# Fused decoder layer: the down projection's sums in three lanes of tiles on ScalarE's queue

## The chip, the cores and the metric

The kernel is one program on one core of a Trainium2 chip. The metric is the device time of one execution in microseconds (us); lower is better. The engines are TensorE (PE in the profile; PEld its weight loads), VectorE (DVE), ScalarE (ACT), GpSimd (POOL) and SyncE (SP). Each engine works through its own instructions in the order in which the program gives them. DMAs are issued by an engine's queue (here nearly all by SP's); the issuing engine passes on to its next instruction when the DMA is out, and a DMA whose data must first be ready holds up what stands behind it on that engine.

## The reference

One decoder layer for T = 1024 tokens of D = 1024 features in fp32:

```python
mod = silu(c) @ w_ada + b_ada                     # six vectors: shift, scale, gate, twice (AdaLN)
u = x * (1 + scale_m) + shift_m
y = mixer(u)                                      # window attention + dilated attention, gated, then @ w_o
x = layer_norm(ALPHA * x + (1 + gate_m) * y)
u = x * (1 + scale_f) + shift_f
h = u @ w_gate_up                                 # 1024 x 5632: hg, hu of 2816 columns each
y = (silu(hg) * hu) @ w_down                      # 2816 x 1024
x = layer_norm(ALPHA * x + (1 + gate_f) * y)
```

The change lies in the last part, from `w_o` (its last residual sums) on.

## The kernel before

**Matrix products.** A product in fp32 is made of three matmuls of split operands (high x high, high x low, low x high). Weights arrive in fp32 by DMA; `split` makes the halves: ScalarE copies to `w_hi` (L144), VectorE subtracts to get `w_lo` (L145). TensorE's matmuls of such a product are at L1037 (`product`, `mac`).

**Stages around the change.** After the attention, the product with `w_o` writes eight banks of PSUM, one for each block of 128 rows, for the first 512 columns; `residual` (L1321) adds `x` to each on VectorE. The needed parts of `x` (tiles `xr`) are loaded by SP: four ahead, and each of the other four (`fetch_x`, L1318) when a `residual` has freed its tile. Then come the other 512 columns, the first layer norm, and the gate-and-up projection.

**Gate and up.** 22 pairs (a block of 128 columns of `hg` and the one of `hu`) are computed with Strassen and Winograd's scheme: seven products of 12 matmuls each instead of eight (the products are steps i = 0 to 6 of the loop over a pair p). Of pairs 0 to 3 two products were made ahead. A pair's weights are two tiles `r1`, `r2` of 512 KB (loaded by SP at L112, two pairs ahead); GpSimd makes sums of them (L126 to L132). `g_prepare(n + 3)` splits the weights of two products ahead. Results go through a few elementwise steps: ScalarE copies a bank (L1604, L1610) and applies Silu (L1616), VectorE adds and multiplies (L1614, L1620, L1621), GpSimd adds (L1618), and SP stores the two halves of the pair's `h` to `h_d` in DRAM (L1623, at i = 6). GpSimd also applies the first norm's `gain` (L1366, L1367) at the end of pairs 3 to 10.

**The sums for the down projection.** It uses the same scheme: seven products of 11 units (j), each unit 12 matmuls (L1655: four banks, three matmuls each). It needs sums of blocks of `w_down` and of `h`: 22 sets, 11 of either kind. A set (`sum_set`) loads two tiles of 512 KB (from `w_down` or from `h_d`, L1514, SP's queue), does four VectorE operations in two steps (L1520 to L1524 for `w_down`, L1526 to L1530 for `h`) and stores the tiles to DRAM (`wt2_d` or `hs_d`, L1534; the trace says `wt_d`, `hs_d`). It is a generator: each `yield` gives the work back until the next product. There are two lanes with tiles of their own, lane 0 with `a_raw` and `a_lo` from pair 8 on, lane 1 with `gb` from pair 11 on:

```python
def sums_ahead(p, i):
    for lane, first in enumerate((8, 11)):
        if i == 1 and p >= first and sets and (sets[0][0] == "w" or 2 * sets[0][1] + 1 < p):
            ...
            lanes[lane] = sum_set(*sets.pop(0), *tiles)
        next(lanes[lane], None)
```

So both lanes start a set at the same step, i = 1, of each pair; the loads go out there, the first two operations come two products later, the other two one later again, and the stores two products after those. One last set is done in the down projection itself.

**AdaLN.** `last_ada` makes the last gate vector in pairs 2 and on: 512 KB of `w_ada` into `a_raw` (L1486, SP), and at the next call VectorE adds it up (L1489, L1491). It is called at four of a pair's seven products.

**Down projection.** A unit's two operands (`dn_load`, 256 KB each, L1562 and L1564, SP) are split (`dn_prepare`; L169 on ScalarE, L170 on VectorE) and multiplied. The raw tiles are the buffers of `r1` and `r2`. In the last pair of gate and up, `dn_prepare(2 * i, ...)` splits the first units at every product from i = 1 on. After each product `dn_add` (L1649 and the line behind it) adds four banks into the rows `zt`, and `half_stats` gathers their statistics. Products 0, 2, 4 and 6 write the same four banks (`bank_a`); 1 has four others, and 3 and 5 share four more. During product 6, the last, the second layer norm is applied to rows 0 to 3 (`norm_shared`, whose second part is the returned `finish`), then to rows 4 to 7 as they get done; `norm_quick(7)` ends the program.

The order of instructions on each engine is that in which this code issues them. In the listings below `waits DMAHW3` means that an instruction waits for one of eight counters by which hardware DMAs report that they have landed; the DMAs take them in turn, whatever queue they are on. `x2` means twice in a row.

Of the kernel before, what the change touches and what calls it, by code (L numbers as in the profile page):

```python
# [18 lines left out]
P = 128  # L19
T = 1024  # L20
# [129 lines left out]
def decoder_layer(ctx: ExitStack, tc: tile.TileContext, I, out, dbg=None):  # L150
# [1165 lines left out]
    def fetch_x(tb, eh, pool):  # L1316
        xr_t[tb, eh] = pool.tile([P, 512], F32, name="xr", tag="half" if eh == 0 else "r", bufs=XB[eh])
        nc.sync.dma_start(xr_t[tb, eh], I["x"][tb * P:(tb + 1) * P, eh * 512:(eh + 1) * 512])  # L1318

    def residual(ps, tb, eh):  # L1320
        nc.vector.scalar_tensor_tensor(zrow(tb)[:, eh * 512:(eh + 1) * 512], xr_t.pop((tb, eh)), ALPHA, ps,  # L1321
                                       op0=OP.mult, op1=OP.add)
# [12 lines left out]
    for tb in range(NB):
        residual(banks[tb], tb, 0)
        if tb + XB[0] < NB:
            fetch_x(tb + XB[0], 0, mix)
    w_late = [ws.take(2) for _ in range(4)]
    ps2x.close()  # L1340
    ph2b.close()
# [140 lines left out]
    def last_ada():  # L1482
        acc5 = misc.tile([P, T], F32, name="gate5", bufs=1)
        for k in range(KC):
            raw = ev.tile([P, T], F32, name="a_raw", bufs=1)
            nc.sync.dma_start(raw, I["w_ada"][k * P:(k + 1) * P, 5 * D:])  # L1486
            yield
            if k == 0:
                nc.vector.tensor_scalar(acc5, raw, c_act[:, 0:1], None, op0=OP.mult)  # L1489
            else:  # L1490
                nc.vector.scalar_tensor_tensor(acc5, raw, c_act[:, k:k + 1], acc5, op0=OP.mult, op1=OP.add)  # L1491
            yield
        hl = [ev.tile([P, T], F32R, name=n, tag=n, bufs=1) for n in ("a_raw", "a_lo")]
        split(*hl, acc5)
        yield
        nc.sync.dma_start(acc5, I["b_ada"][:, 5 * D:].to_broadcast([P, D]))
        yield
        for t in range(2):
            s = slice(t * TH, (t + 1) * TH)
            ps = ps_x.tile([P, TH], F32, name="px")  # L1500
            for x in range(2):
                nc.tensor.matmul(ps, ones_r, hl[x][:, s], start=x == 0, stop=x == 1)
            nc.vector.tensor_tensor(acc5[:, s], ps, acc5[:, s], op=OP.add)
        nc.vector.tensor_scalar(acc5, acc5, 1.0, None, op0=OP.add)
        gates[5] = acc5

    ada = last_ada()
    NP = NF // 2
    sets = [(kind, j) for kind in "wh" for j in range(NP)]

    def sum_set(kind, j, x, y):
        for i, tile in enumerate((x, y)):
            f = 2 * j + i
            nc.sync.dma_start(tile, I["w_down"][f * P:(f + 1) * P, :] if kind == "w" else h_d[f])  # L1514
        yield
        yield
        x0, x1, y0, y1 = x[:, H0], x[:, H1], y[:, H0], y[:, H1]
        tt = nc.vector.tensor_tensor
        if kind == "w":
            tt(x0, x1, x0, op=OP.subtract)  # L1520
            tt(x1, y1, x1, op=OP.subtract)
            yield
            tt(y1, y1, x0, op=OP.subtract)
            tt(y0, y0, y1, op=OP.subtract)  # L1524
        else:
            tt(y1, x1, y1, op=OP.add)  # L1526
            tt(x1, x0, x1, op=OP.subtract)
            yield
            tt(x0, y1, x0, op=OP.subtract)
            tt(y0, y0, x0, op=OP.subtract)  # L1530
        yield
        yield
        for i, tile in enumerate((x, y)):
            nc.sync.dma_start((wt2_d if kind == "w" else hs_d)[j, 2 * i:2 * i + 2].rearrange("s p c -> p s c"),  # L1534
                              tile.rearrange("p (s c) -> p s c", s=2))
        yield

    lanes = [iter(()), iter(())]

    def sums_ahead(p, i):  # L1540
        for lane, first in enumerate((8, 11)):
            if i == 1 and p >= first and sets and (sets[0][0] == "w" or 2 * sets[0][1] + 1 < p):
                if lane == 0:
                    tiles = [ev.tile([P, T], F32, name=n, tag=n, bufs=1) for n in ("a_raw", "a_lo")]
                else:
                    gb = misc.tile([P, 2, D], F32, name="gb", tag="gb")
                    tiles = [gb[:, 0], gb[:, 1]]
                lanes[lane] = sum_set(*sets.pop(0), *tiles)
            next(lanes[lane], None)
# [4 lines left out]
    def dn_load(upto):  # L1554
        while len(dn_raw) < min(upto, DN):
            u = len(dn_raw)
            i, j = divmod(u, NP)
            raw = gx.tile([P, 2, TH], F32, name="dn", tag="r1" if u % 2 else "r2", bufs=2)
            dn_raw[u] = raw
            f = 2 * j + (i in (1, 5, 6))  # L1560
            rows = slice(f * P, (f + 1) * P)
            nc.sync.dma_start(raw[:, 0], {0: h_d[f][:, H0], 1: h_d[f][:, H0], 2: hs_d[j, 0], 3: hs_d[j, 3], 4: hs_d[j, 1],  # L1562
                                          5: hs_d[j, 2], 6: h_d[f][:, H1]}[i])
            nc.sync.dma_start(raw[:, 1], {0: I["w_down"][rows, H0], 1: I["w_down"][rows, H0], 2: wt2_d[j, 3], 3: wt2_d[j, 0],  # L1564
                                          4: wt2_d[j, 1], 5: I["w_down"][rows, H1], 6: wt2_d[j, 2]}[i])
# [10 lines left out]
    for p in range(NF):  # L1576
# [11 lines left out]
        for i in range(7):  # L1588
# [42 lines left out]
            else:  # L1631
                if i == 0:
                    dn_load(2)
                dn_prepare(2 * i, 2 if i < 4 else 4)
            sums_ahead(p, i)
            if p == 3 and i == 0:
                gb1 = norm_params(1)
            if p > 1 and i in (1, 3, 4, 6):
                next(ada, None)
            if i == 6 and 3 <= p < 3 + NB:  # L1640
                gain(p - 3, gb1)
# [18 lines left out]
        bst[tb] = st8[:, tb * 12:(tb + 1) * 12].rearrange("p (a b) -> p a b", a=2)  # L1660
    bank_a = [ps_f.tile([P, TH], F32, name="pf") for _ in range(4)]
    bank, ends = None, []
    last_set = sum_set(*sets.pop(0), *[ev.tile([P, T], F32, name=n, tag=n, bufs=1) for n in ("a_raw", "a_lo")])
    for i in range(6):
        if i in (1, 3):
            bank = [(ps_f, ps_x)[t // 2].tile([P, TH], F32, name=("pf", "px")[t // 2]) for t in range(4)]
        ps = bank if i % 2 else bank_a
        for j in range(NP):
            u = i * NP + j
            dn_prepare(u + 12, 4)  # L1670
            for t in range(4):
# [103 lines left out]
```

## Time and profile before

| | before |
|---|---|
| three runs, us | 1856.27, 1852.13, 1851.0 (median 1852.13) |
| profiled execution, us | 1854.48 |
| its span, us; mean granted clock | 1852.7; 0.982 |
| PE busy | 1783.3 (96%), 8774 matmuls |
| DVE, ACT, POOL busy | 1214.1 (66%), 843.3 (46%), 562.9 (30%) |
| DMA | 277.28 MB, 150 GB/s on average |
| chain that ended last | PE 73%, DVE 11%, DMA 7%, issue 3%, ACT 3%, SP's queue 2% |

The span runs from the first to the last recorded instruction; the execution's time holds some 2 us more. "Busy" counts an engine's own instructions, not the issuing of DMAs. The granted clock is the share of TensorE's full clock that it was allowed. The residual behind `w_o` lies near 1083 us of the span, pairs 3 to 21 of gate and up from 1199.65 to 1624.08, the down projection from there to 1833.5, and the last norms end at 1852.7. Rows of the trace give a time, a duration, engine, line and operation with output <- inputs; in brackets stands how long the engine had idled ahead of it and what ended that.

### The profile page before, as it was taken

How to read it: one execution, taken by the hardware profiler on the slowest of the kernel's cores; microseconds unless marked ns; L12 is line 12 of the kernel's file. 1: busy time of each engine (PE TensorE's matmuls, PEld its weight loads, DVE VectorE, ACT ScalarE, POOL GpSimd, SP SyncE). 2: the span in 40 equal slices, each digit the busy share in tenths (PEclk: the TensorE clock that was granted, in tenths of full speed). 3: DMA queues.
4: the chain of work that ended last, by engine and by line, in shares of the span. 5: the costliest groups of instructions: out<-in, count | busy, mean ns of one | idle time of the engine just before them, and what ended most of it. 6: DMA issues, size and time to landing. Idle time of an engine off the chain costs nothing.

```text
span 1852.7 us, 24551 instructions
## 1 busy us (share of the span) xinstructions
PE 1783.3 (96%) x8774; PEld 1458.4 (79%) x8774; DVE 1214.1 (66%) x2094; ACT 843.3 (46%) x1731; POOL 562.9 (30%) x357
## 2 busy tenths in 40 slices
PE   9999999999999999999999999999998889799995
PEld 7888888888888888788888878878777767688884
DVE  7655566557657766478558757766766666557668
ACT  6554444444445777654522227533333333344332
POOL 0232223323332322045026532456642223200003
PEclk9999999999999999999999999999999999899998
DMA  9322233234233322375756340343456666587542
GB/s 354 90 78 84 82 87 103 82 82 120 71 92 103 88 86 70 103 269 187 239 207 218 120 142 12 131 143 114 137 206 254 241 233 237 171 280 241 195 144 91
DMA packets 124058, 277.28 MB, mean 150 GB/s; under 512 B 17888, under 2 KB 27680, under 8 KB 123936
## 3 DMA queue, kind: packets, MB, share of 16 engines
q1 hardware_dynamic: 123328, 274.06, 44.3%
q8 instruction: 69, 1.13, 0.2%
q0 software_dynamic: 464, 1.58, 0.2%
q14 instruction: 53, 0.43, 0.1%
q10 hardware_dynamic: 144, 0.07, 0.0%
HBM read 203.99 MB, written 58.03 MB: 141 GB/s over the span
## 4 chain that ended last, share of the span: by engine, by line
PE 73%; DVE 11%; DMA 7%; issue 3%; ACT 3%; SPq 2%; POOL 1%; DVEq 0%; ACTq 0%; POOLq 0%
PE pf L1037 9%; PE pj L191 8%; PE pj L193 8%; PE pj L192 8%; PE pf L1655 7%; PE p L1037 6%; PE s L623 4%; PE p L191 3%; PE p L193 3%; PE p L192 3%; PE po L684 3%; PE pt L661 2%; PE px L1655 2%; DVE w_lo L145 2%; DMA a_lo<-h_d 1%
## 5 line engine op out<-in xcount | busy, mean ns | idle before, releaser
L191 PE MATMUL pj<-u,w_hi 128*128 128x512 f32 x736 | 302.5, 411 | 0.0
L193 PE MATMUL pj<-u,w_lo 128*128 128x512 f32 x736 | 288.6, 392 | 0.0
L192 PE MATMUL pj<-u,w_hi 128*128 128x512 f32 x736 | 288.0, 391 | 0.0
L550 POOL TENSOR_TENSOR rb<-rb,sin_t 128x512 f32<-128x512 f32 x64 | 85.7, 1339 | 519.3 <-DVE rb L548 484.6
L79 DVE TENSOR_TENSOR w_lo<-w_raw,w_hi 128x512 fp32r<-128x512 f32 x132 | 125.6, 954 | 79.3 <-ACT w_hi L78 78.9
L145 DVE TENSOR_TENSOR w_lo<-r,w_hi 128x512 fp32r<-128x512 f32 x128 | 131.2, 1030 | 67.6 <-ACT w_hi L144 67.2
L1655 PE MATMUL pf<-dn 128*128 128x512 f32 x726 | 170.1, 389 | 0.0
L191 PEld LDWEIGHTS pj<-u,w_hi 128*128 128x128 f32 x736 | 138.5, 188 | 31.7 <-issue 6.2
L193 PEld LDWEIGHTS pj<-u,w_lo 128*128 128x128 f32 x736 | 138.1, 188 | 30.7
L639 ACT ACTIVATE probs<-probs,st 128x128 f32<-128x128 f32 (+1 forms) x320 | 145.6, 461 | 30.9 <-DVE st L628 30.6
L1655 PEld LDWEIGHTS pf<-dn 128*128 128x128 f32 x726 | 136.4, 188 | 28.4
L192 PEld LDWEIGHTS pj<-u,w_hi 128*128 128x128 f32 x736 | 138.8, 189 | 22.4
L169 ACT ACTIVATE dn<-dn 128x1024 fp32r<-128x1024 f32 x77 | 81.7, 1061 | 113.8 <-DMA dn<-in_w_down 40.8
L170 DVE TENSOR_TENSOR dn<-dn 128x1024 fp32r<-128x1024 f32 x77 | 92.5, 1222 | 53.8 <-ACT dn L169 52.7
L78 ACT ACTIVATE w_hi<-w_raw 128x512 fp32r<-128x512 f32 x132 | 81.7, 622 | 92.5 <-PE p L192 55.0
L551 POOL TENSOR_TENSOR r<-ra,rb 128x512 f32<-128x512 f32 x63 | 115.9, 1839 | 4.9
L663 ACT ACTIVATE ptsb<-pt 128x512 f32<-128x512 f32 (+1 forms) x128 | 63.5, 549 | 100.5 <-PE pt L661 100.2
L1616 ACT ACTIVATE g<-g 128x512 f32<-128x512 f32 x39 | 24.7, 632 | 166.4 <-DVE g L1614 166.4
L126 POOL TENSOR_TENSOR s<-r 128x512 f32<-128x512 f32 x27 | 36.4, 1347 | 170.0 <-DVE w_lo L145 137.6
L564 ACT ACTIVATE qs<-r 64x1024 fp32r<-64x1024 f32 x38 | 40.2, 1058 | 101.2 <-POOL r L551 100.7
L565 DVE TENSOR_TENSOR qs<-r,qs 64x1024 fp32r<-64x1024 f32 x38 | 46.4, 1220 | 57.2 <-ACT qs L564 56.5
L623 PE MATMUL s<-kh,qs 128*128 128x256 f32 (+1 forms) x320 | 79.7, 283 | 2.1 <-DVE st L628 1.8
(409 smaller groups left out, 4386.1 us busy)
## 6 DMA issues: line engine op xcount, KB each, us to landing
w_raw<-in_w_in SPq DMA_DIRECT2D x100, 256.0 KB
r<-in_w_gate_up SPq DMA_DIRECT2D x44, 512.0 KB
a_raw<-in_w_ada SPq DMA_DIRECT2D x32, 512.0 KB
dn<-hs_d SPq DMA_DIRECT2D x44, 256.0 KB
dn<-wt_d SPq DMA_DIRECT2D x44, 256.0 KB
h_d<-g SPq DMA_DIRECT2D x39, 256.0 KB
dn<-h_d SPq DMA_DIRECT2D x33, 256.0 KB
dn<-in_w_down SPq DMA_DIRECT2D x33, 256.0 KB
```

The costliest lines, as they stand in the source:

```text
L79: self.nc.vector.tensor_tensor(lo, raw, hi, op=OP.subtract)
L145: self.nc.vector.tensor_tensor(lo, src, hi, op=OP.subtract)
L170: nc.vector.tensor_tensor(lo, src, hi, op=OP.subtract)
L191: nc.tensor.matmul(ps, w[0], m[0], start=first, stop=False)
L192: nc.tensor.matmul(ps, w[0], m[1], start=False, stop=False)
L193: nc.tensor.matmul(ps, w[1], m[0], start=False, stop=last)
L550: eng.tensor_tensor(b, b, sin_t[:, s], op=OP.mult)
L551: eng.tensor_tensor(residue_half(res, r, t), by_residue(a, r), by_residue(b, r), op=OP.add)
L623: nc.tensor.matmul(pss[h][:, i, lo:], box["q"][h][:, b * P:(b + 1) * P], ks[h][:, (b - 1 + lo) * P:(b + 1) * P], start=i == 0 and n == 0, ...
L639: nc.scalar.activation(pr, pr, AF.Exp, scale=-1.0, bias=st[:, 0, h, b:b + 1], accum_out=st[:, 1, h, b:b + 1])
L1037: nc.tensor.matmul(ps, w[:, c], m[:, k], start=first and k == 0 and n == 0, stop=k == 3 and n == 2, skip_group_check=True)
L1655: nc.tensor.matmul(ps, op[:, x, 0, c], op[:, y, 1], start=first and n == 0, stop=last and n == 2, skip_group_check=True)
```

## The change

1. The sums use three lanes: lane 0 from pair 4 on with three tiles of the weights' pool (`w_raw`) and one more (`s3`, printed as `s_12285` below); lane 1 (`a_raw`, `a_lo`) from pair 8; lane 2 (`gb`) from pair 11. A lane begins a new set as soon as its last one is through, at any product; lanes 0 and 2 begin none from pair 20 on, lane 1 goes on into the down projection.
2. A set's loads are four DMAs of 256 KB on ScalarE's queue instead of two of 512 KB on SP's. Five products pass until the first operations (before: two), and four after the stores (before: one). The stores are four plain 256 KB DMAs on SP's queue.
3. `last_ada` loads on ScalarE's queue, with three products until the use, and is called at every product.
4. The seven products of the down projection come in the order 0, 1, 2, 3, 5, 4, 6. The norms of rows 0 to 3 are issued during product 4 instead of 6.
5. In the last pair the units are split from i = 3 on (two there, then two more with each product), not from i = 1 on.
6. The last four `x` tiles for the residual of the first 512 columns are loaded ahead into tiles that are free by then (`fetch_pair`), not after a `residual`.

```diff
+    def fetch_pair(tb, tag):
+        pair = mix.tile([P, T], F32, name="xr2", tag=tag, bufs=2)
+        for i in range(2):
+            xr_t[tb + i, 0] = pair[:, i * 512:(i + 1) * 512]
+            nc.sync.dma_start(xr_t[tb + i, 0], I["x"][(tb + i) * P:(tb + i + 1) * P, :512])
...
     for kp in range(4):
+        if kp in (1, 2):
+            fetch_pair(2 * kp + 2, ("o_raw", "gt")[kp - 1])
...
         residual(banks[tb], tb, 0)
-        if tb + XB[0] < NB:
-            fetch_x(tb + XB[0], 0, mix)
...
-            nc.sync.dma_start(raw, I["w_ada"][k * P:(k + 1) * P, 5 * D:])
+            nc.scalar.dma_start(raw, I["w_ada"][k * P:(k + 1) * P, 5 * D:])
+            yield
+            yield
             yield
...
+    ORDER = (0, 1, 2, 3, 5, 4, 6)
...
-        for i, tile in enumerate((x, y)):
+        for i, halves in enumerate((x, y)):
             f = 2 * j + i
-            nc.sync.dma_start(tile, I["w_down"][f * P:(f + 1) * P, :] if kind == "w" else h_d[f])
-        yield
-        yield
+            src = I["w_down"][f * P:(f + 1) * P, :] if kind == "w" else h_d[f]
+            for t in range(2):
+                nc.scalar.dma_start(halves[t], src[:, t * TH:(t + 1) * TH])
+        for _ in range(5):
+            yield
...
-        for i, tile in enumerate((x, y)):
-            nc.sync.dma_start((wt2_d if kind == "w" else hs_d)[j, 2 * i:2 * i + 2].rearrange("s p c -> p s c"),
-                              tile.rearrange("p (s c) -> p s c", s=2))
-        yield
+        for i, tile in enumerate((x0, x1, y0, y1)):
+            nc.sync.dma_start((wt2_d if kind == "w" else hs_d)[j, i], tile)
+        for _ in range(4):
+            yield
...
+        for lane, first in enumerate((4, 8, 11)):
+            if lanes[lane] and next(lanes[lane], "end") == "end":
+                lanes[lane] = None
+            if (not lanes[lane] and (p, i) > (first, 0) and p < (20, NF + 1, 20)[lane] and sets
+                    and (sets[0][0] == "w" or 2 * sets[0][1] + 1 < p)):
+                lanes[lane] = sum_set(*sets.pop(0), *lane_tiles(lane))
+                next(lanes[lane])
...
-                dn_prepare(2 * i, 2 if i < 4 else 4)
+                if i >= 3:
+                    dn_prepare(2 * i - 4, 4)
...
-            if p > 1 and i in (1, 3, 4, 6):
+            if p > 1:
                 next(ada, None)
...
-    last_set = sum_set(*sets.pop(0), *[ev.tile([P, T], F32, name=n, tag=n, bufs=1) for n in ("a_raw", "a_lo")])
-    for i in range(6):
+    for n, i in enumerate(ORDER[:-1]):
...
-            next(last_set, None)
+            sums_ahead(NF, 1)
+            if i == 4:
+                if 1 <= j < 9 and j % 2:
+                    ends.append(norm_shared(j // 2, gb2, out))
+                elif 1 <= j < 9:
+                    ends.pop(0)()
...
-            if j == 5:
-                for _ in range(2 if t < 2 else 0):
-                    ends.append(norm_shared(todo.pop(0), gb2, out))
-                while len(ends) > 1:
-                    ends.pop(0)()
```

**The sums' loads.** SP's queue before, around the start of pair 12; `r_...` are a pair's raw weights:

```order
L1534 DMA wt_d<-a_lo 128x2x512 [waits DMAHW6_49]
L1534 DMA wt_d<-gb 128x2x512 [waits DMAHW7_49]
L1534 DMA wt_d<-gb 128x2x512 [waits DMAHW0_49]
L1514 DMA a_raw<-in_w_down 128x1024 [waits DMAHW5_49,DMAHW1_49]
L1514 DMA a_lo<-in_w_down 128x1024 [waits DMAHW6_49,DMAHW2_49]
L1514 DMA gb<-in_w_down 128x1024 [waits DMAHW7_49,DMAHW3_49,DMAHW0_49]
L1514 DMA gb<-in_w_down 128x1024 [waits DMAHW4_49]
L112 DMA r_12478<-in_w_gate_up 128x1024 [waits DVE_49]
```

ScalarE's instructions now, in pair 11 (`s_...` are GpSimd's sums of a pair's weights, but `s_12285` is the tile `s3`):

```order
L1625 ACTIVATE g<-pf 128x512 [waits DMAHW2_49,PE_49]
L1525 DMA w_raw<-in_w_down 128x512 [waits DMAHW7_49,DMAHW5_49]
L1525 DMA w_raw<-in_w_down 128x512 [waits DMAHW6_49,DMAHW1_49]
L1525 DMA w_raw<-in_w_down 128x512 [waits DMAHW3_49]
L1525 DMA s_12285<-in_w_down 128x512 [waits DMAHW4_49,DMAHW0_49]
L144 ACTIVATE w_hi<-s_12167 128x512 [waits Activation_49]
L1637 ACTIVATE g<-g 128x512 [waits DVE_49]
L1525 DMA gb<-in_w_down 128x512 [waits DMAHW5_49,Pool_49]
L1525 DMA gb<-in_w_down 128x512 [waits DMAHW6_49]
L1525 DMA gb<-in_w_down 128x512 [waits DMAHW7_49]
L1525 DMA gb<-in_w_down 128x512 [waits DMAHW0_49]
L144 ACTIVATE w_hi<-r_12057 128x512 [waits Activation_49]
```

Four issues of a set now stand on ScalarE between a pair's own instructions, ahead of a copy to `w_hi`, and here two lanes load in neighbouring products. (Lines of the changed file are some 20 higher: L1625 is L1604 of before, L1637 is L1616.)

**The sums on VectorE.** Before, in pair 11, the operations of both lanes together:

```order
L145 TENSOR_TENSOR w_lo<-s_12270,w_hi 128x512
L1614 TENSOR_TENSOR g<-g,pf 128x512
L145 TENSOR_TENSOR w_lo<-r_12159,w_hi 128x512
L145 TENSOR_TENSOR w_lo<-r_12158,w_hi 128x512
L1520 TENSOR_TENSOR a_raw<-a_raw 128x512
L1521 TENSOR_TENSOR a_raw<-a_lo,a_raw 128x512
L1520 TENSOR_TENSOR gb<-gb 128x512
```

Now, at the end of pair 11 and the start of pair 12:

```order
L1641 TENSOR_TENSOR g<-g,pf 128x512
L1642 TENSOR_TENSOR g<-g,c_12376 128x512
L1534 TENSOR_TENSOR s_12285<-s_12285,w_raw 128x512
L1535 TENSOR_TENSOR w_raw<-w_raw,s_12285 128x512
L1531 TENSOR_TENSOR gb<-gb 128x512
L1532 TENSOR_TENSOR gb<-gb 128x512
L145 TENSOR_TENSOR w_lo<-s_12337,w_hi 128x512
L1534 TENSOR_TENSOR gb<-gb 128x512
L1535 TENSOR_TENSOR gb<-gb 128x512
L145 TENSOR_TENSOR w_lo<-s_12336,w_hi 128x512
```

The operations of a set are the same four; they moved from a fixed place in the pair to wherever a lane's counting puts them, here behind a pair's last multiplications.

**The last pair on ScalarE.** Before, with `dn` the units of the down projection:

```order
L1616 ACTIVATE g<-g 128x512 [waits DVE_49]
L169 ACTIVATE dn<-dn 128x1024 [waits DMAHW4_49,DMAHW3_49]
L169 ACTIVATE dn<-dn 128x1024 [waits DMAHW6_49,DMAHW5_49]
L144 ACTIVATE w_hi<-r_13601 128x512 [waits DMAHW0_49,Activation_49,Pool_49]
L1604 ACTIVATE g<-pf 128x512 [waits DMAHW2_49,PE_49]
L169 ACTIVATE dn<-dn 128x1024 [waits DMAHW7_49,DMAHW0_49]
L169 ACTIVATE dn<-dn 128x1024 [waits DMAHW2_49,DMAHW1_49]
L144 ACTIVATE w_hi<-r_13600 128x512 [waits Pool_49]
```

Now:

```order
L1637 ACTIVATE g<-g 128x512 [waits DVE_49]
L144 ACTIVATE w_hi<-r_13704 128x512 [waits DMAHW2_49,Activation_49,Pool_49]
L1625 ACTIVATE g<-pf 128x512 [waits PE_49]
L144 ACTIVATE w_hi<-r_13703 128x512 [waits Pool_49]
L1631 ACTIVATE c_13978<-pf 128x512 [waits PE_49]
L169 ACTIVATE dn<-dn 128x1024 [waits DMAHW4_49,DMAHW3_49]
L169 ACTIVATE dn<-dn 128x1024 [waits DMAHW6_49,DMAHW5_49]
L144 ACTIVATE w_hi<-r_13704 128x512 [waits Activation_49]
```

The units' splits moved behind two more of the pair's own copies to `w_hi`; one of these still follows them.

More of the change, by code (lines that the diff above doesn't have):

```diff
@@ L1508, in decoder_layer @@
     NP = NF // 2
+    ORDER = (0, 1, 2, 3, 5, 4, 6)
     sets = [(kind, j) for kind in "wh" for j in range(NP)]
     def sum_set(kind, j, x, y):
-        for i, tile in enumerate((x, y)):
+        for i, halves in enumerate((x, y)):
             f = 2 * j + i
-            nc.sync.dma_start(tile, I["w_down"][f * P:(f + 1) * P, :] if kind == "w" else h_d[f])
-        yield
-        yield
-        x0, x1, y0, y1 = x[:, H0], x[:, H1], y[:, H0], y[:, H1]
+            src = I["w_down"][f * P:(f + 1) * P, :] if kind == "w" else h_d[f]
[3 more added lines that the diff above has]
+            yield
+        (x0, x1), (y0, y1) = x, y
         tt = nc.vector.tensor_tensor
@@ L1532, in sum_set, with lane_tiles @@
         yield
-        for i, tile in enumerate((x, y)):
-            nc.sync.dma_start((wt2_d if kind == "w" else hs_d)[j, 2 * i:2 * i + 2].rearrange("s p c -> p s c"),
-                              tile.rearrange("p (s c) -> p s c", s=2))
-        yield
-    lanes = [iter(()), iter(())]
-    def sums_ahead(p, i):
[L1541 to L1549, printed above, removed]
+        for i, tile in enumerate((x0, x1, y0, y1)):
+            nc.sync.dma_start((wt2_d if kind == "w" else hs_d)[j, i], tile)
+        for _ in range(4):
+            yield
+    lanes = [None] * 3
+    def lane_tiles(lane):
+        if lane == 0:
+            tiles = [wpool.tile([P, TH], F32, name="w_raw", tag="w_raw", bufs=3) for _ in range(3)]
+            tiles.append(gx.tile([P, TH], F32, name="s3", bufs=1))
+            return tiles[:2], tiles[2:]
+        if lane == 1:
+            tiles = [ev.tile([P, T], F32, name=n, tag=n, bufs=1) for n in ("a_raw", "a_lo")]
+        else:
+            gb = misc.tile([P, 2, D], F32, name="gb", tag="gb")
+            tiles = [gb[:, 0], gb[:, 1]]
+        return [[x[:, H0], x[:, H1]] for x in tiles]
+    def sums_ahead(p, i):
+        for lane, first in enumerate((4, 8, 11)):
[5 more added lines that the diff above has]
+                next(lanes[lane])
     dn_raw, dn_op = {}, {}
@@ L1556, in dn_load @@
             u = len(dn_raw)
-            i, j = divmod(u, NP)
+            i, j = ORDER[u // NP], u % NP
             raw = gx.tile([P, 2, TH], F32, name="dn", tag="r1" if u % 2 else "r2", bufs=2)
@@ L1668, in decoder_layer @@
         for j in range(NP):
-            u = i * NP + j
+            u = n * NP + j
             dn_prepare(u + 12, 4)
@@ L1680, in decoder_layer @@
     dn_prepare(DN, 4)
-    todo = list(range(4))
     for t in range(4):
```

## The prediction

> **What bounds the kernel.** I read the page's slices first, then windows over the stretches that the change touches, then the waits inside the slow one.
>
> ```profile
> PE   9999999999999999999999999999998889799995
> 1199.65:1624.08 424.43, 383.06 (x1577) 307.19 (x1577) 274.69 (x307) 143.58 (x250) 173.98 (x108) 0.95 0.55 193
> 1624.08:1833.53 209.45, 209.45 (x925) 173.08 (x923) 144.62 (x168) 81.98 (x82) 11.35 (x5) 1.00 0.57 195
> 1280.00:1300.00 20.00, 20.00 (x90) 16.58 (x89) 11.24 (x13) 7.30 (x13) 12.93 (x8) 1.00 0.23 80
> 1400.00:1420.00 20.00, 18.45 (x74) 15.14 (x75) 12.14 (x17) 6.83 (x13) 3.83 (x3) 0.91 0.67 240
> 1480.00:1500.00 20.00, 16.40 (x68) 13.08 (x68) 11.26 (x14) 4.95 (x9) 7.10 (x5) 0.94 0.78 280
> 1600.00:1620.00 20.00, 10.54 (x27) 6.75 (x28) 10.24 (x9) 10.41 (x13) 1.30 (x1) 0.76 0.54 177
> 1655.38 1.36 PE px L1655 x6
> ```
>
> TensorE is the bound, and it is full everywhere but in one place. Columns: stretch, length, then busy time and count of PE, weight loads, DVE, ACT, POOL, then the granted clock, the DMA share and GB/s. Six matmuls take 1.36 us when nothing waits, so a product of 12 takes 2.72. The down projection (second window) has 925 matmuls in 209.45 us, 0.2264 each: no stall. The stretch from 1199.65 to 1624.08, pairs 3 to 21 of the gate-and-up projection, has 1577 in 424.43. At 0.2267 they need 357.4; **67.0 us** are lost there, which the 20 us windows show as 68 to 74 matmuls, and 27 at the end, instead of 90. Who waited for whom, from 1155 to 1620:
>
> ```profile
> PE pf L1037 <- DVE w_lo L145: 32.3, 15, 4.0
> PE pf L1037 <- ACT g L1604: 4.6, 1, 4.6
> DVE a_lo L1526 <- DMA a_lo<-h_d: 24.6, 6, 5.0
> DVE a_raw L1520 <- DMA a_raw<-in_w_down: 14.4, 6, 4.8
> DVE gate L1491 <- DMA a_raw<-in_w_ada: 4.3, 1, 4.3
> ACT dn L169 <- DMA dn<-in_w_down: 14.0, 7, 5.3
> ```
>
> PE waits for `w_lo`, the last step of preparing a product's weights. DVE makes it late because it stands, in its own order, behind an instruction that waits for a load: of a set of sums (24.6 + 14.4 us), of AdaLN (4.3), and ScalarE behind loads of the down projection's units in the last pair (14.0). One pair (12) in full:
>
> ```profile
> 1388.71 5.89 DMA wt_d<-gb
> 1395.00 5.11 DMA gb<-in_w_down
> 1390.07 1.20 SPq L1514 DMA_DIRECT2D a_raw<-in_w_down  x1
> 1396.24 1.33 DVE L1520 TENSOR_TENSOR a_raw<-a_raw 128x512 f32<-128x512 f32 x1 [4.78 <-DMA a_raw<-in_w_down]
> 1401.55 0.50 PE L1037 MATMUL pf<-t4h,w_lo 128*128 128x512 f32 x1 [3.36 <-DVE w_lo L145]
> 1403.47 0.63 PE L1037 MATMUL pf<-t4l,w_hi 128*128 128x512 f32 x1
> 1407.89 0.93 SPq L1623 DMA_DIRECT2D h_d<-g  x2
> 1431.28 0.93 SPq L1623 DMA_DIRECT2D h_d<-g  x2
> ```
>
> The set's loads leave SP only after the stores of the set before it have left the same tiles (5.89 us), land some 5 us later, and DVE wanted them after two products. PE stands 3.36 us and then runs slow matmuls (0.63 for 0.39; clock 0.91 in that window). Pairs follow each other at 23.39 us instead of 7 x 2.72 = 19.04: 4.35 lost per pair.
>
> **The change, part by part.**
> *Sums.* The same 22 sets (2 MB in and out, four DVE operations each) come from pair 4 on in three lanes of tiles; loads go out on ScalarE's queue, a new set's after its lane's stores have had four products, and DVE uses them five products after their issue: 13.6 us for a flight of about 5.1. So the 39.0 us of DVE's waits for them go, with the slow clock behind them. The cover is that margin; with 1.75 sets per pair and a pair's own 1.5 MB, pairs 11 to 19 move 5.2 MB in 19.04 us, 275 GB/s, which the 280 GB/s window carried at a share of 0.78.
> *AdaLN loads.* Also on ScalarE's queue, three products ahead instead of one: 4.3 us of wait gone.
> *What ScalarE pays.* 96 more issues. The one issue that it makes now took 0.40, so a set costs it 1.6 us in one step, and a pair 2.8 us of an engine that is busy 7.3 of 20. What counts is lateness:
>
> ```profile
> 0.74 0.40 ACTq L164 DMA_DIRECT2D ident<-in_k_ident  x1
> 1392.34 0.60 ACT L1610 ACTIVATE c<-pf 128x512 f32<-128x512 f32 x1 [1.60 <-PE pf L1037]
> 1392.84 0.62 ACT L144 ACTIVATE w_hi<-r 128x512 fp32r<-128x512 f32 x1
> 1390.77 0.69 DVE L145 TENSOR_TENSOR w_lo<-r,w_hi 128x512 fp32r<-128x512 f32 x1 [1.10 <-ACT w_hi L144]
> ```
>
> A copy starts when a product ends (1392.34), the next `w_hi` follows, `w_lo` takes 0.69, and PE wants the pair two products after that end: 5.44 - (0.50 + 0.62 + 0.69) leaves 3.6 us. Behind the issues wait exactly this `w_hi`, then DVE, then PE. 1.6 fits. But an issue also waits until the DMA eight places earlier has landed (the counters DMAHW0 to 7 in the order), and at five places (pairs 11, 12, 14, 16, 17) two lanes load in neighbouring steps, so a load waits for one issued a step before, 4.8 us of flight at most by the last pair's first loads (below). Bounds: nothing, or the 4.35 of a pair today; I take 1 us each, 5 in all, since most of the flight lies under the 2.72 between the steps and the 3.6.
> *What DVE pays.* Twelve sum operations fall into six steps, then six steps have none: 12 x 0.69 + 7 x 0.69 + 5 x 0.69 = 16.6 us in 16.3, before GpSimd slows it:
>
> ```profile
> 1212.33 5.60 DVE L145 TENSOR_TENSOR w_lo<-r,w_hi 128x512 fp32r<-128x512 f32 x2
> 1211.29 3.32 POOL L1366 TENSOR_TENSOR zt<-zt,gb 128x1024 f32<-128x1024 f32 x1
> ```
>
> Beside a GpSimd operation the same `w_lo` took 2.8 us. Five such bursts less the 3.6 of margin: 0 to 4.35 each; I take 1, and 2 for pairs 4 to 10, where sums now meet GpSimd's gain. **Left over: 12 us of the 67.0** (0 to 10 x 4.35 + 2 = 45).
> *Last pair.*
>
> ```profile
> 1594.53 0.96 SPq L1562 DMA_DIRECT2D dn<-h_d  x1
> 1597.34 4.79 DMA dn<-in_w_down
> 1600.89 1.06 ACT L169 ACTIVATE dn<-dn 128x1024 fp32r<-128x1024 f32 x1 [5.26 <-DMA dn<-in_w_down]
> 1603.17 0.61 ACT L144 ACTIVATE w_hi<-r 128x512 fp32r<-128x512 f32 x1
> ```
>
> Units are split from the second product on, while their loads are just leaving; `w_hi` stands behind. Now the first two are split at the fourth product, three products after their loads, and only the last `w_hi` follows. Later units still wait, but nothing of this pair's weights does. At the down projection's start two units are ready instead of eight; a unit needs 2.72 on PE, 1.06 on ACT and 1.23 on DVE, so supply outruns use: 0, at most the 14.0 of today. These waits are inside the 67.0.
> *x for the residual.* Loaded ahead into spare tiles:
>
> ```profile
> 1082.72 1.49 DVE L1321 SCALAR_TENSOR_TENSOR zt<-xr,p 128x512 f32<-128x512 f32 x2 [0.65 <-DMA xr<-in_x]
> 1083.56 0.47 PE L191 MATMUL pf<-o_hl,m 128*128 128x512 f32 x1 [2.20 <-DVE zt L1321]
> 1087.49 0.63 PE L193 MATMUL pf<-o_hl,m 128*128 128x512 f32 x1
> ```
>
> Of 2.20 remain the 0.3 or so by which the seventh residual ends after PE; with it go eight slow matmuls (0.43 apart for 0.23): 1.9 + 1.6 = 3.5 saved, 1.9 if the clock still falls.
> *Order 5 before 4, and the early norms.* Product 5 now follows 3 on the same banks, 6 follows 4 on the same:
>
> ```profile
> 1743.11 0.68 DVE L1649 TENSOR_TENSOR g<-pf,gate 128x512 f32<-128x512 f32 x1
> 1745.76 0.68 DVE L1649 TENSOR_TENSOR g<-px,gate 128x512 f32<-128x512 f32 x1
> 1829.75 3.79 PE L1655 MATMUL pf<-dn 128*128 128x512 f32 x16
> 1801.61 0.69 DVE L1649 TENSOR_TENSOR g<-pf,gate 128x512 f32<-128x512 f32 x1 [3.80 <-PE pf L1655]
> 1840.99 0.68 DVE L1649 TENSOR_TENSOR g<-pf,gate 128x512 f32<-128x512 f32 x1
> ```
>
> DVE empties banks every 1.33 us (1743.11, fourth 1745.76), PE refills one per 0.68: from a product end at 1743.8 the fourth bank is 0.9 late. Before 6, PE does a whole bank in 7.5 us: no wait. In exchange rows 0 to 3 are normalized during 4. Today that work fills DVE at the end: PE ends at 1833.5, but the last bank is read at 1840.99, 7.5 us later, where another (1801.61) is read as soon as it is full. What follows (to 1852.7) stays. Saved 7.4 (0 if DVE is behind for another reason).
>
> **Sum.** -67.0 + 12 - 3.5 + 0.9 - 7.4 = -65.0. The profiled execution took 1854.48, span 1852.7; the median of the three runs is 1852.13, and I subtract from that: **1787**.
>
> The Trainium skill ("TensorE: Matmul & The Clock Gate", Part 1) lets the clock fall only after an idle window of about 3.4 us. By it each residual stall under 3.4 would cost its idle time alone, and my 12 could be some 9: 1784. The trace differs: the 2.20 us wait at 1083.56 was followed by 0.63 matmuls.
>
> **Rivals.** *ScalarE becomes the waiter:* in pairs 11 to 19 its issues wait for landings so long that each pair loses the 4.35 again: 39 for my 10, 1816. For it: stores flew 5.89. Against: most loads have four products behind the store. *The last pair's wait stays,* with the first loads still behind SP's stores: +14, 1801. *The loads come no sooner:* only the issuing queue changed, the flights queue at a share near 0.8, and DVE's 39 us stay with half as much slow clock (59): 1787 + 59 - 12 = 1834. The Trainium skill ("Trainium Kernel Development and Optimization", Key Constraints) says this: DMAs from all queues share 16 engines, and another queue saves only issue time. Against it here is the longer lead, 13.6 for 5.4. *Slower:* every set's first issue meets its lane's stores in flight: 5.89 - 3.6 = 2.3 plus 1.6 of slow clock, with four DMAs each blocked in turn (0.4 x 4): 5.5 x 21 sets = 116, so 1776 + 116 = 1892. It decides against the change from 3.6 us per set; SP would have to send stores more than 5 us late every time.
>
> **Numbers.** Forecast case 0.72 (own range 1775 to 1802), ScalarE waits 0.10, last pair 0.07, no sooner 0.07, slower 0.03, no visible difference 0.01. Low end 1775: no stall left at all (1775.1). High end 1815: residue near its bound, or the last pair's and part of ScalarE's. Anything within 0.3% (5.6 us, about what a measurement tells from no change): 0.01; faster 0.96, slower 0.03.
>
> **What would show it.** Waits of DVE for `in_w_down`, `h_d` and `in_w_ada` near zero; 131 products in about 370 us instead of 424; DMA issues on ACT of 0.4 us and some of several, with PE gaps behind these alone; no PE gap in the last pair; first `pf` matmul within 0.5 us of the last `p`; last bank read within 1 us of PE's end. I am wrong if ACT idles for DMA in most pairs, or if the DMA share passes 0.9 there.

## Result and the profile after

| | before | after |
|---|---|---|
| runs, us | 1856.27, 1852.13, 1851.0, 1852.21, 1851.3 | 1811.52, 1808.98, 1809.36, 1811.13, 1811.64 |
| median, us | 1852.13 | 1811.13 |
| span of the profiled execution, us | 1852.7 | 1809.7 |

The ratio is 0.9773 (95% interval 0.9759 to 0.9787): faster by 41 us, where 65 were forecast.

The page of the changed kernel, engines and slices; the dip of PE has moved to the last slices:

```profile
span 1809.7 us, 24697 instructions
PE 1766.1 (98%) x8774; PEld 1446.2 (80%) x8774; DVE 1218.5 (67%) x2094; ACT 844.0 (47%) x1731; POOL 570.1 (32%) x357
PE   9999999999999999999999999999999999999977
```

Windows over the stages that answer to the two of before (columns as there), and three short ones that are used below:

```profile
1195.00:1572.16 377.16, 365.10 (x1577) 295.07 (x1576) 270.61 (x302) 140.03 (x244) 179.18 (x108) 1.00 0.60 210
1572.16:1798.00 225.84, 212.06 (x925) 174.40 (x923) 159.28 (x185) 89.22 (x90) 17.93 (x6) 0.97 0.58 198
1273.60:1277.00 3.40, 2.64 (x12) 2.17 (x12) 3.37 (x7) 0.00 (x0) 0.00 (x0) 1.00 0.37 138
1487.00:1490.40 3.40, 3.40 (x9) 2.64 (x9) 2.75 (x5) 0.52 (x2) 0.00 (x0) 0.50 0.69 229
1757.00:1770.00 13.00, 3.79 (x9) 3.05 (x10) 11.18 (x11) 3.55 (x4) 3.25 (x1) 0.50 0.20 81
```

Taken from the starts of the first and last matmuls of these stages, the change of the span comes apart into four terms. Their sum is the difference of the two profiled spans, 43.0; the medians differ by 41.0.

| stage | before, us | after, us | difference | forecast |
|---|---|---|---|---|
| to pair 3's first full product | 1199.5 | 1195.0 | -4.5 | -3.5 |
| pairs 3 to 21 | 424.4 | 377.2 | -47.2 | -55.0 |
| down projection | 209.2 | 225.8 | +16.6 | +0.9 |
| from its last matmul to the end | 19.6 | 11.7 | -7.9 | -7.4 |

The first and last did about what was forecast, the second fell 7.8 us short of it, and the third is where most of the missing gain went. Some waits of VectorE, TensorE and ScalarE in the stretch that was read before, 1155 to 1620, which now takes in the first 48 us of the down projection (rows: who waits, for what, us in all, times, longest):

```profile
DVE gate L1499 <- DMA a_raw<-in_w_ada: 2.4, 1, 2.4
PE pf L1037 <- DVE w_lo L145: 8.9, 9, 2.0
ACT w_hi L144 <- DMA wt_d<-a_raw: 7.4, 2, 5.0
```

No row of VectorE for `in_w_down` or `h_d` is left, where the two largest had 39.0 us (all of them 48.7); one wait for `w_ada` stays. TensorE waits 8.9 us for `w_lo` instead of 32.3. New are waits of ScalarE's copies behind issues that could not leave; the row shown, for a store of sums, is one of them.

The hole: a gap of TensorE at the step from product 4 to product 6 of the down projection. Its row, and those of the other engines ahead of it (start, duration, engine, line; in brackets the idle time ahead and what ended it):

```profile
1766.21 9.00 PE L1677 MATMUL pf<-dn 128*128 128x512 f32 x30 [13.37 <-DVE g L1671]
...
1729.12 2.34 DVE L170 TENSOR_TENSOR dn<-dn 128x1024 fp32r<-128x1024 f32 x2
...
1732.24 0.16 DVE L1295 SCALAR_TENSOR_TENSOR brs<-bmv,brs 128x1 f32<-128x1 f32 x1
...
1737.10 3.32 POOL L1300 TENSOR_TENSOR zt<-zt,gb 128x1024 f32<-128x1024 f32 x1 [167.95 <-DVE zt L1299]
1738.93 1.50 DVE L1295 SCALAR_TENSOR_TENSOR brs<-bmv,brs 128x1 f32<-128x1 f32 x1
1742.69 1.23 DVE L170 TENSOR_TENSOR dn<-dn 128x1024 fp32r<-128x1024 f32 x1 [2.26 <-ACT dn L169]
...
1748.50 1.24 ACT L1296 ACTIVATE zt<-zt,brs 128x1024 f32<-128x1024 f32 x1 [1.77 <-DVE brs L1295]
1749.65 1.99 ACT L169 ACTIVATE dn<-dn 128x1024 fp32r<-128x1024 f32 x2
1750.73 1.23 DVE L170 TENSOR_TENSOR dn<-dn 128x1024 fp32r<-128x1024 f32 x1 [2.26 <-ACT dn L169]
...
1760.96 4.50 DVE L170 TENSOR_TENSOR dn<-dn 128x1024 fp32r<-128x1024 f32 x2
1765.39 0.68 DVE L1671 TENSOR_TENSOR g<-pf,gate 128x512 f32<-128x512 f32 x1
```

Product 4 was through on TensorE at 1752.8. Its first bank was read at 1765.39: VectorE stands in its order, and ahead of that reading stood all the unit splits and the four norms. One norm with two splits takes 8.0 us (1742.69 to 1750.73), TensorE uses two units in 5.4. In each round VectorE idles 2.26 us for a split's first half on ScalarE (L169), which stands there behind a normalization (L1296) that waits for VectorE's small steps (L1295). So 13.4 us are lost, and more at the lower clock that follows (0.50 until 1770).

### The profile page after: what moved, and what is told of

The parts are those of the page before. It is cut to its first block, busy times and chain, and to the rows that moved or that the text cites. A ratio compares the mean times of both kernels' runs of the same rounds, so it can differ in the third digit from the quotient of the medians.

```text
span 1809.7 us, 24697 instructions
## 1 busy us (share of the span) xinstructions
PE 1766.1 (98%) x8774; PEld 1446.2 (80%) x8774; DVE 1218.5 (67%) x2094; ACT 844.0 (47%) x1731; POOL 570.1 (32%) x357
## 4 chain that ended last, share of the span: by engine, by line
PE 85%; DVE 8%; issue 3%; ACT 2%; DMA 1%; POOL 1%; ACTq 0%; DVEq 0%; SPq 0%; POOLq 0%
PE pf L1037 16%; PE pj L191 9%; PE pj L193 9%; PE pj L192 9%; PE pf L1677 7%; PE p L1037 6%; PE s L623 4%; PE p L191 3%; PE p L193 3%; PE p L192 3%; PE po L684 3%; PE pt L661 3%; PE px L1677 2%; DVE w_lo L145 1%; PE pf L191 1%
## 5 line engine op out<-in xcount | busy, mean ns | idle before, releaser
L145 DVE TENSOR_TENSOR w_lo<-r,w_hi 128x512 fp32r<-128x512 f32 x128 | 135.2, 1065 | 85.9 <-ACT w_hi L144 82.1
L1677 PE MATMUL pf<-dn 128*128 128x512 f32 x726 | 172.3, 392 | 13.4 <-DVE g L1671 13.4
L169 ACT ACTIVATE dn<-dn 128x1024 fp32r<-128x1024 f32 x77 | 80.7, 1058 | 81.5 <-DMA dn<-wt_d 30.7
L144 ACT ACTIVATE w_hi<-r 128x512 fp32r<-128x512 f32 x128 | 79.5, 623 | 32.4 <-DMA h_d<-g 6.3
L1300 POOL TENSOR_TENSOR zt<-zt,gb 128x1024 f32<-128x1024 f32 x7 | 20.3, 2895 | 214.6 <-DVE zt L1299 214.6
```

Of the source, the lines that this page charges most:

```text
L145: self.nc.vector.tensor_tensor(lo, src, hi, op=OP.subtract)
L1677: nc.tensor.matmul(ps, op[:, x, 0, c], op[:, y, 1], start=first and n == 0, stop=last and n == 2, skip_group_check=True)
```

## Experiments

Theories are named in the expectations. Times are medians; a ratio is to the kernel before in the same round.

**Norms back into product 6.** Edit, against the changed kernel:

```diff
-            if i == 4:
-                if 1 <= j < 9 and j % 2:
-                    ends.append(norm_shared(j // 2, gb2, out))
-                elif 1 <= j < 9:
-                    ends.pop(0)()
```
(and the old lines back in product 6)

> The changed kernel with one part undone: the norms of rows 0 to 3 are again issued in product 6, the last; the order 0, 1, 2, 3, 5, 4, 6 stays. Theory 'VectorE late': the 13.4 us hole in TensorE ahead of product 6 comes from the norms inside product 4, which hold VectorE's unit splits and behind them the reading of product 4's banks. Then the hole falls to about 1 us, the end is late again by 7.5, and the time is 1811 - 15.6 + 7.5 = 1803. Rival 'same banks': product 6 waits because it follows 4 on the same banks, norms or not. Then the hole stays near 13 us and the late end comes on top: 1818.

1802.15 us (0.9723, 0.9708 to 0.9737). The down projection takes 210.2 us from its first matmul to its last, and the hole is gone (its window, and VectorE's reading of the last bank):

```profile
1571.30:1781.90 210.60, 210.15 (x925) 173.09 (x923) 152.25 (x175) 87.17 (x87) 11.40 (x5) 1.00 0.61 208
```
```profile
1789.33 0.68 DVE L1671 TENSOR_TENSOR g<-pf,gate 128x512 f32<-128x512 f32 x1
```

That reading comes 7.4 us after TensorE's end at 1781.9, as in the kernel before. "VectorE late" holds: the early norms cost 15.6 us in one place (225.8 against 210.2) to save 7.4 in another.

**Also the old order of products:** `ORDER = (0, 1, 2, 3, 4, 5, 6)`.

> As the run before, and the order of the seven products back to 0 to 6. Both theories: no hole ahead of product 6, since product 5 lies between 4 and 6; the end late by 7.5; 1802. 'VectorE late' says that this is the same as the run before within 2 us, 'same banks' that it is 13 to 16 us faster than it.

1802.03 us (0.9721, 0.9707 to 0.9736): no difference from the run above beyond the noise. The rival "same banks" is out. By the traces the order itself costs 1 us (down projection 210.2 against 209.2), as forecast (0.9).

**Norms in product 4, small steps of all four rows together.**

```diff
-                if 1 <= j < 9 and j % 2:
-                    ends.append(norm_shared(j // 2, gb2, out))
+                if j == 0:
+                    rows4 = scales(range(4))
+                elif 1 <= j < 9 and j % 2:
+                    ends.append(norm_shared(j // 2, gb2, out, rows4[j // 2]))
```
(`scales`, a new function, does mean, variance, square root and scale of the given rows; `norm_shared` then takes them from it)

> The changed kernel with the norms still in product 4, but the small steps (mean, variance, square root, scale) of all four rows done together at its first unit, so that later units' copies on ScalarE no longer stand behind a normalization that waits for VectorE's small steps. 'VectorE late': VectorE's own work in product 4 is 8.2 (four banks read) + 13.4 (11 splits) + 4.9 (four multiplications) + about 3, some 29.5 us against 29.9 of TensorE; the hole falls from 13.4 to 0 to 5 us, the end stays early: about 1798 (1794 to 1803). 'Same banks': hole unchanged, 1811.

1804.89 us (0.9735, 0.972 to 0.9749): half of what I expected. The long waits for ScalarE are gone, but a hole of 6.4 us stays. VectorE's rows and TensorE's say why:

```profile
1737.99 4.57 DVE L170 TENSOR_TENSOR dn<-dn 128x1024 fp32r<-128x1024 f32 x2
1760.09 32.18 PE L1692 MATMUL pf<-dn 128*128 128x512 f32 x132 [6.44 <-DVE g L1686]
```

Each row's last step is an addition on GpSimd (3.3 us). Two splits take 4.57 us beside it and 2.34 otherwise (1729.12 above): 2.2 us for each of four rows, 8.9 in all. I had counted VectorE's work without this.

**The last pair's old places for the units' splits:** `dn_prepare(2 * i, 2 if i < 4 else 4)` for the `if i >= 3` line.

> The changed kernel with the last pair's splits of the first down projection units back at the old place (from the second product on). If the old place was what made ScalarE and behind it TensorE wait: three waits of some 4 us with slow matmuls come back in the last pair, 1811 + 14 = 1825 (up to 1829). If the lighter queue of SP alone cured it: 1811, no gap in the last pair.

1823.77 us (0.9838, 0.9821 to 0.9855): 12.6 slower than the changed kernel, as expected. Pair 21 loses 12.3 us again; ScalarE waits for the units' loads with `w_hi` behind it.

```profile
ACT dn L169 <- DMA dn<-in_w_down: 11.2, 7, 3.1
```

**Lane 2 one pair later:** `enumerate((4, 8, 12))` for `(4, 8, 11)`.

> The changed kernel with one number changed: lane 2 starts after pair 12's first product instead of pair 11's (4, 8, 12 for 4, 8, 11). By the order of the code no two lanes then load in neighbouring products, and no three products in a row hold more than one set's operations. Of the 19.8 us of stall that pairs 3 to 21 keep, I read about 4 behind DMA issues that wait on ScalarE and about 7 behind bursts of sums on VectorE. Theory 'neighbours': these 11 go, 1811 - 11 = 1800 (1798 to 1803). Rival 'load on the DMA engines or GpSimd': they stay, 1811.

1801.73 us (0.9717, 0.9697 to 0.9738), 9.4 faster than the changed kernel. Pairs 3 to 21 take 367.4 us instead of 377.2. "Neighbours" holds, but this run moves two things, the issues and the bursts on VectorE. One issue that waits is not enough to stop TensorE: here too three issues hold ScalarE in pair 11, the copy behind them waits 5.1 us, and TensorE is busy for 7.90 of the 8 us around it.

```profile
1358.73 0.63 ACT L144 ACTIVATE w_hi<-s 128x512 fp32r<-128x512 f32 x1 [5.12 <-DMA wt_d<-a_raw]
```
```profile
1358.00:1366.00 8.00, 7.90 (x35) 6.14 (x35) 4.80 (x5) 3.97 (x8) 4.17 (x3) 1.00 0.56 177
```

**The sums' loads back on SP's queue**, all else kept: `nc.sync.dma_start(halves[t], ...)`.

> The changed kernel with the sums' loads back on SP's queue, all else kept (three lanes, lead of five, halves). Theory 'lead': the queue does not matter, VectorE still waits for no load, and the 4 us of waiting issues on ScalarE go: 1805 to 1811. Rival 'queue': SP's loads stand behind its stores and its waits for h, VectorE waits for loads again, 20 us or more: 1831 or more.

1801.75 us (0.9716, 0.9695 to 0.9737): more than the 4 us expected. Here the bursts on VectorE stand where the changed kernel has them, and the stall of pairs 11 to 21 is nearly gone, 2.7 us against 12.9. So the bursts alone do not make the stall; and in the run before, which keeps the issues on ScalarE, they alone do not either (3.2 left). By these two runs it takes both, a set's issues close to another set's issues and operations. The changed kernel's rows of ScalarE's queue and engine, first a set whose issues meet no wait (0.82 and 0.93 for four), then two neighbours:

```profile
1297.74 0.82 ACTq L1525 DMA_DIRECT2D a_raw<-in_w_down  x2
1298.60 0.93 ACTq L1525 DMA_DIRECT2D a_lo<-in_w_down  x2
...
1352.76 4.67 ACTq L1525 DMA_DIRECT2D w_raw<-in_w_down  x3
1357.88 0.34 ACTq L1525 DMA_DIRECT2D s<-in_w_down  x1
1358.26 0.63 ACT L144 ACTIVATE w_hi<-s 128x512 fp32r<-128x512 f32 x1 [4.96 <-DMA wt_d<-a_raw]
1360.31 1.81 ACTq L1525 DMA_DIRECT2D gb<-in_w_down  x4
1362.17 0.63 ACT L144 ACTIVATE w_hi<-r 128x512 fp32r<-128x512 f32 x1 [1.29 <-issue]
```

Three issues hold the engine for 4.67 us, until another lane's store has landed; the copy that TensorE needs stands behind, and the next set's four follow at once. With the loads on SP, nothing that they hold up costs TensorE more than the 2.7 us. VectorE still waits for no load of a set, so leaving SP's queue was not what brought them in time.

**Two products of lead instead of five:** `range(2)` for `range(5)` ahead of the first operations, `range(7)` for `range(4)` behind the stores.

> The changed kernel with two products instead of five between a set's loads and its first operations (the three go behind the stores, so that sets start where they did). Theory 'lead': the five products are what took VectorE's waits for these loads away (39 us in the kernel before, with two products of lead); a flight of some 5 us behind up to 1.8 us of issuing no longer fits into 5.4, VectorE waits again for in_w_down and h_d, and 15 to 45 us come back: 1826 to 1856. Rival 'tiles': it is enough that a load no longer stands behind the store that empties its tiles; two products do, 1811 to 1817.

1813.35 us (0.9784, 0.9759 to 0.9808): 2 us from the changed kernel, within the spread of its runs (1811.6 to 1818.0). Gate and up takes 378.0 us. The theory "lead", on which my prediction rested, falls: VectorE's longest row of waits for a set's loads is 1.8 us for `h_d`.

```profile
1195.60:1573.60 378.00, 363.49 (x1578) 294.13 (x1577) 273.09 (x302) 140.03 (x244) 178.97 (x108) 1.00 0.61 210
```
```profile
DVE a_lo L1537 <- DMA a_lo<-h_d: 1.8, 2, 1.1
```

**The kernel before, with the sums' and AdaLN's loads on ScalarE's queue and nothing else** (L1514, L1486: `nc.scalar` for `nc.sync`).

> The kernel before with one thing changed: the loads of the sums and of AdaLN go out on ScalarE's queue; two lanes, tiles, leads and all else as before. Theory 'tiles': the loads still wait until the stores have left the same tiles (5.9 us for one), so VectorE still waits for them, and the issues now hold ScalarE's copies up as well: 1853 to 1890. Rival 'queue': leaving SP's queue is what brings the loads forward: 1833 or less.

1864.37 us (1.0048, 1.003 to 1.0065): slower. The queue alone takes most of the waits from VectorE and gives them to ScalarE, which stands behind its own issues until the stores have left the tiles:

```profile
1199.00:1633.60 434.60, 384.44 (x1577) 306.55 (x1576) 264.74 (x308) 142.95 (x250) 174.10 (x108) 0.94 0.54 188
```
```profile
1392.98 0.63 ACT L144 ACTIVATE w_hi<-r 128x512 fp32r<-128x512 f32 x1 [8.47 <-DMA a_lo<-in_w_down]
1394.15 0.79 PE L1037 MATMUL pf<-t3h,w_hi 128*128 128x512 f32 x1 [5.59 <-ACT g L1604]
```

Compare the run with two products of lead: the same queue and the same lead, but there the eight loads of two sets leave ScalarE in 4.2 us (1390.72 to 1394.94), where here four of twice the size take 7.1 (1385.78 to 1392.88); and pairs 3 to 21 take 378.0 us there, 434.6 here, of which the last pair explains some 16. So neither ScalarE's queue nor the longer lead was needed for the gain of gate and up; no run went without both at once. What the good versions share, and this run lacks, is the room between a lane's stores and the next loads into its tiles (four products or more, against two), with the third lane that allows it, and DMAs of half the size. Which of these counts is not shown: no run changed one alone.

**Without GpSimd's gain** (the first norm's gain and bias in pairs 3 to 10 are left out).

> The changed kernel without GpSimd's gain and bias of the first norm in pairs 3 to 10 (this work is left out, so its time is no version's). Theory 'GpSimd': of the 19.8 us left in gate and up, 7 to 9 come from VectorE's operations that take 2.3 to 2.9 us instead of 0.69 beside these GpSimd operations, now that sums are made there too: 1802 to 1804, and no TensorE gap over 0.5 us before pair 11. Rival: the sums' own operations fill VectorE there: 1809 to 1811.

1801.96 us (0.9716, 0.9691 to 0.9741). The stall of pairs 3 to 10 falls from 7.9 to 1.7 us; the rest of the gain lies in pairs 11 to 21 (12.9 to 9.0). Of that, 2.3 us lie in pair 11, into which the work of pair 10 reaches (GpSimd's row at 1351.10 below). The other 1.6 lie in pair 17: TensorE waits 1.93 us there (at 1478.57) and the clock stays at 1.00, where the changed kernel's wait of 2.03 us is followed by 3.4 us at half the clock. Rows of the changed kernel at the end of pair 4, and at the start of pair 11 (from 1349.8):

```profile
1230.28 2.74 POOL L1373 TENSOR_TENSOR zt<-zt,gb 128x1024 f32<-128x1024 f32 x1
1230.67 0.67 DVE L1641 TENSOR_TENSOR g<-g,pf 128x512 f32<-128x512 f32 x1
1231.27 2.30 DVE L1642 TENSOR_TENSOR g<-g,c 128x512 f32<-128x512 f32 x1
1233.49 0.68 DVE L1531 TENSOR_TENSOR w_raw<-w_raw 128x512 f32<-128x512 f32 x1
...
1351.10 2.72 POOL L1373 TENSOR_TENSOR zt<-zt,gb 128x1024 f32<-128x1024 f32 x1
1351.49 2.87 DVE L145 TENSOR_TENSOR w_lo<-r,w_hi 128x512 fp32r<-128x512 f32 x1
1354.42 0.50 PE L1037 MATMUL pf<-b21h,w_lo 128*128 128x512 f32 x1 [1.31 <-DVE w_lo L145]
```

Beside GpSimd's operation, the one that reads two tiles (`g`, `c`) takes 2.30 us, the one that reads a tile and a bank (`g`, `pf`) 0.67, and the next one behind it 0.68. Sums that are moved into these pairs find VectorE already late.

**A version with the mends:** loads on SP's queue, lane 2 from pair 12, small steps together, two rows' last steps in product 4 (at j = 2 and 4) and two in product 6.

> The changed kernel with three mends together: the sums' loads on SP's queue, lane 2 starting at pair 12, and the norms of rows 0 to 3 spread (small steps of all four at product 4's first unit, the last multiplication and GpSimd's addition of two rows in product 4, of two in product 6). If the stall of pairs 11 to 21 is ScalarE's issues and the hole is VectorE's lateness, 9.4 (as with SP's queue alone) and 14 to 15.6 go: 1811 - 24.5 = 1786 (1783 to 1790), no TensorE gap over 1 us behind 1570 us but that ahead of product 5's third bank, and the end within 12 us of TensorE's last matmul. If the two mends of the loads hold the same stall, lane 2 adds nothing to SP's queue.

1790.44 us (0.9644, 0.9628 to 0.9659), 4 us short of it. Gate and up took 365.9 us, 1.0 less than with SP's queue alone: the two mends of the loads do hold the same stall. In the down projection a hole of 3.0 us stayed.

**The same with the first norm's gain on VectorE** (`nc.vector.tensor_tensor` at i = 2 and 4, one operation each).

> The run before, with the first norm's gain and bias in pairs 3 to 10 as two VectorE operations (1.22 us each, at the third and fifth product) instead of GpSimd's two. If GpSimd's operations cost by slowing VectorE's neighbours (9 us by the run without them), 2.4 us of VectorE per pair is cheaper, and some 5 us go: 1781 (1778 to 1785). If VectorE has no room in pairs 4 to 10, beside sums and AdaLN, stalls of the same size stay: 1786 or more.

1783.83 us (0.9605, 0.9587 to 0.9622): 6.6 faster; pairs 3 to 10 lose 2.5 us instead of 7.8. VectorE had room for 2.4 us a pair, not for GpSimd beside it. The hole ahead of product 6 had another cause in this version, which SP's waits and ScalarE's rows show:

```profile
SPq L1316 <- POOL zt L1315: 6.5, 2, 3.7
```
```profile
1729.07 1.06 ACT L169 ACTIVATE dn<-dn 128x1024 fp32r<-128x1024 f32 x1 [5.46 <-DMA dn<-wt_d]
```

A finished row's store waits on SP for GpSimd's addition, and the loads of the last units stand behind it.

**One row's last steps at j = 8 of product 4, three in product 6:** `elif j == 8: ends.pop(0)()`.

> The last version (sums' loads on SP's queue, lane 2 from pair 12, small steps together, first norm's gain on VectorE), with one row's last steps in product 4, behind its last unit loads, and three rows' in product 6. There the hole ahead of product 6 was still 3.2 us: ScalarE waited 5.5, 1.7 and 0.6 us for units' loads, which stood on SP behind two stores of finished rows that waited 3.7 and 2.8 us for GpSimd. If that is the cause, the hole falls under 1 us, and VectorE has room for one more row in product 6 (it idled 5.4 us between its banks): 1783.8 - 5 = 1779 (1777 to 1781). If VectorE's own work is the cause, 2 us of hole stay: 1782. If product 6 has no room, the end comes late by the row's 2 to 4 us: 1781 to 1784.

1778.51 us (0.9589, 0.9573 to 0.9604), as expected. This beats both kernels; by the two ratios it takes 1.9% less time than the changed one (0.9589 / 0.9773). TensorE works at the full clock from gate and up to its end:

```profile
1195.00:1553.00 358.00, 357.56 (x1574) 294.92 (x1573) 261.95 (x317) 138.72 (x244) 133.92 (x92) 1.00 0.65 221
1553.00:1766.00 213.00, 210.19 (x925) 173.10 (x923) 161.97 (x188) 89.36 (x90) 17.02 (x6) 1.00 0.63 211
```

## Why the prediction was right, and where not

Direction and range held (1811.13 in 1775 to 1815); the likeliest case's own range, 1775 to 1802, did not. By its steps:

- *Sums and AdaLN: the waits for loads go.* Right, but for 2.4 us of AdaLN's. The reason given, a lead of 13.6 us for a flight of 5.1, was not needed: with two products of lead (5.4 us) the time was 2.2 us longer, within its spread. That this term came out is in part luck: the cover that I counted was the lead, and the room behind the stores, which the prediction names without a price, came with the same edit.
- *Last pair.* Right: 0.1 us of stall left in pair 21, and 12.6 us come back with the old places. The down projection started without a wait, as priced.
- *Left over, 12 us of the 67.0.* Mis-sized: 19.8 (377.2 - 357.4; by 2.72 us for each product it is 7.9 in pairs 3 to 10 and 12.9 behind). The 5 us for ScalarE's issues measured 10.3 (377.2 against 366.9 with SP's queue), where they meet a neighbouring set's. The stalls of pairs 11 to 21 lie in pairs 11, 13, 15 and 17, 2.3 to 4.0 us each, where I had put 1 us each at 11, 12, 14, 16 and 17. The bound named for an issue was right, one that waits for a landing 4.8 us away (4.67 measured); what failed was "most of the flight lies under the 2.72 between the steps and the 3.6". The 5 us for bursts on VectorE is at most the 2.7 that SP's queue left. The 2 us for GpSimd in pairs 4 to 10 measured 6.2 (7.9 to 1.7), and 2.3 more in pair 11: I had seen the 2.8 us operation and priced its collisions too low.
- *x for the residual.* 3.5 forecast, 4.5 measured from the stages; TensorE's gap at that place fell from 2.20 to 0.19 us. No run undid this part alone.
- *Order 5 before 4.* 0.9 forecast, 1.0 measured.
- *"In exchange rows 0 to 3 are normalized during 4 ... Saved 7.4."* This is the step that failed. The 7.9 us at the end were saved, but I wrote down what the norms leave at the end and not what they find where they go. VectorE in product 4 already has four banks to read (8.2 us) and 11 splits (13.4) in TensorE's 29.9; four norms with their waits for ScalarE, and product 6 waiting for product 4's banks at the end of that list, cost 15.6 us. The moved instructions were all in the code, and the same rule that priced the sums, what stands behind them in the engine's order, was not applied to them.
- *Rivals.* "ScalarE becomes the waiter" was partly so, a quarter of its price: 10.3 us of 39; copies to `w_hi` waited for a landing in 8 of the 19 pairs. "The loads come no sooner" is out, since VectorE waits for no load of a set. "Slower" is out for this change, but its mechanism is real: it is what made the run with the queue alone slower.
- *The clock.* The prediction doubted what the Trainium skill ("TensorE: Matmul & The Clock Gate", Part 1) states, that only an idle window of about 3.4 us lowers it. After TensorE's two longest waits in gate and up the short windows above differ: behind 2.03 us at 1486.01 the clock is 0.50 for 3.4 us, behind 1.75 at 1274.36 it stays 1.00. So a wait of 2 us was enough here, and the trace differs from the page. The length alone does not decide it either: in the run with the last pair's old places the clock stayed at 1.00 behind a wait of 2.07 us (at 1486.41), in the run with the small steps together it fell behind 1.78 (at 1486.95). The rows of the changed kernel:

```profile
1274.36 0.50 PE L1037 MATMUL pf<-b21h,w_lo 128*128 128x512 f32 x1 [1.75 <-DVE w_lo L145]
...
1486.01 0.50 PE L1037 MATMUL pf<-t3h,w_lo 128*128 128x512 f32 x1 [2.03 <-DVE w_lo L145]
```

## What to carry to other kernels

When work is moved off the end of a program, price it in the list of the engine at its new place, with what stands behind it there, not only at the old one. Put DMA issues that may have to wait on a queue with nothing urgent behind it: 84 issues of the sums' loads on a ScalarE that was busy 37% of the stretch cost 10 us, since those of two sets came close together. A load that comes too late is not always a matter of queue or lead: look first whether its tile is free.

## What the runs showed of the hardware

In these traces an operation of VectorE that reads two tiles, and begins while GpSimd adds or multiplies two of its own, ends only behind GpSimd's. All sixteen that began beside the gain of pairs 3 to 10 in the changed kernel ended 0.55 us after GpSimd's operation, whenever they began (the one of 2.30 us above at 1233.57, GpSimd's at 1233.02); the nine that read one tile and a bank took 0.67 or 0.68. A step of one column that reads two tiles took 1.50 us in place of 0.16 (1738.93 and 1732.24 above) and ended with GpSimd's at 1740.4. So the price is what is left of GpSimd's operation, 1.6 to 2.2 us in these rows (0.68 to 2.30; two splits 2.34 to 4.57). Doing the gain on VectorE, with 2.4 us more of its own work per pair, was 6.6 us faster. And four issues of 256 KB take ScalarE 1.75 us where nothing holds them (0.82 + 0.93), and 5.0 us where they wait for a landing (4.67 + 0.34).
